# Low parts of all weights by a negated copy and a DMA that adds the weights from DRAM, low-part matmuls last, small first loads on other queues

## The chip, the cores and the metric

The kernel runs on one core of a Trainium2 chip. The metric is the device time of one execution in microseconds, the median of several runs. The profile is of one further execution.

## The reference

Two layers of a hybrid backbone are computed, for 128 context tokens and 512 latent tokens together (640 columns). Each layer modulates and normalises its input, projects it once to 11264 columns, and feeds four branches: a depthwise convolution of width 31, a Hyena long convolution, a pooling mixer and grouped-query attention.

```python
mod = jax.nn.silu(cond) @ p['w_ada'] + p['b_ada']
shift, scale, gate = jnp.split(mod, 3, axis=-1)
h = rms_norm(x, p['norm_g']) * (1.0 + scale) + shift
u = h @ p['w_in']
...
ya = (ya * jax.nn.silu(a_gate)) @ p['wo_conv']
yb = (yb * jax.nn.silu(b_gate)) @ p['wo_hyena']
yc = (yc * jax.nn.silu(c_gate)) @ p['wo_pool']
yd = (att * jax.nn.silu(d_gate)) @ p['wo_attn']
gm = jax.nn.sigmoid(g_merge).reshape(B, L, N_BRANCH, D_MODEL)
merged = gm[:, :, 0] * ya + gm[:, :, 1] * yb + gm[:, :, 2] * yc + gm[:, :, 3] * yd
return x + gate * (merged @ p['w_out'])
```

All inputs and outputs are float32.

## The kernel before

**Precision.** Every float32 operand of a large matmul is kept as two float32r parts, a high part (a rounded copy) and a low part (the operand minus its high part). A product takes three matmuls for each block of 128 rows: high weight with high activation, high weight with low activation, low weight with high activation. `proj` (L383) does that for a column weight: its output has the weight's 128 columns on the partitions and 320 of the 640 tokens, so `both` calls it twice for each weight. `token_proj` (L412) does it the other way round, with tokens on the partitions, for keys, values, queries and the output projection.

**Weights.** `weights` (L331) brings one weight: SyncE's queue loads it into a raw tile (`raw`, two buffers of 512 KB), ScalarE copies it rounded into `whi`, and the low part goes to `wlo` (three buffers each of `whi` and `wlo`). A flag, `pooled[0]`, chooses how. When it is false, VectorE subtracts (`raw` minus `whi`). When it is true, ScalarE writes minus `whi` into `wlo`, and a DMA issued by GpSimd adds `raw` to it. The flag is false for the first three weights of layer 0 (L1811, then true from L1825), true through the Hyena, attention and convolution inputs, and false from the end of the convolution's LayerNorm (`norm`, L1646) to the end of the layer (L1882, L1889). In one execution there are 272 such weights: 168 of eight 128x128 blocks, 56 of four, 40 of four blocks by 256 columns for `token_proj`, and 8 single blocks of the pooling branch. A weight of eight blocks takes 48 matmuls of 320 columns, one of four blocks 24.

**Order of work.** TensorE's order is written out by a small planner, `Loom` (L76): the branches are generators, each `yield` lets another one place its matmuls, and a model of the engines' times decides which goes next. The model only sets the order; it waits for nothing. The other engines' instructions are ordered by the framework's scheduler by priority, those of `weights` 120 instructions ahead (`WAHEAD`). Each engine's queue runs in order. The main line of a layer (`layers`, L1799) is: Hyena inputs and gates, values, keys, queries, the Hyena merge, convolution inputs, pooling inputs, the attention merge, the pooling branch's gates (an eight-block weight alternates with a single block), the pooling merge, the convolution's gates, the convolution's merge, and the output projection. In a merge a column weight of `w_in` (eight blocks) alternates with a column of the branch's own output weight (four blocks, eight for attention). Beside it run threads for the Hyena filters and convolutions, whose elementwise work is on VectorE, ScalarE and GpSimd.

**The start.** Before the planner runs, all first loads are issued on SyncE's queue in the order of the string `DORD`: digits are the eight chunks of `w_ada` (1 MB each, in two halves), `x` the tokens, `t` the Hyena tables, `f` to `i` filter parts. Nineteen small loads, the list `small` (seven of the filter network, the selector, ten parameter rows, one edge table), are dealt in between by `load_small` (L1929). `load` (L324) also gives the planner an estimate of each arrival.

Of the kernel before, what the change touches and what calls it, by code (L numbers as in the profile page):

```python
# [10 lines left out]
F32R = mybir.dt.float32r  # L11
I32 = mybir.dt.int32
AF = mybir.ActivationFunctionType
ALU = mybir.AluOpType
# [14 lines left out]
NSLOT = 13  # L29
NRAW = 2  # L30
NHI = 3
DORD = "0sf4xt15gh2637"
SMALL = 3
PT = 6.5
PN = 4.0
HW = 80
# [30 lines left out]
def r32(ap):  # L67
    return ap.bitcast(F32)
# [165 lines left out]
def hybrid_flow_backbone(ctx: ExitStack, tc: tile.TileContext, i, o):  # L234
    nc = tc.nc
# [85 lines left out]
            dve.scalar_tensor_tensor(out=lo, in0=src, scalar=scale, in1=r32(hi),  # L321
                                     op0=ALU.mult, op1=ALU.subtract)

    def load(dst, src):  # L324

        sp.dma_start(out=dst, in_=src)  # L326
        lm.issue = max(lm.issue, lm.pe - 2.0) + 0.48
        lm.dma = max(lm.dma, lm.issue + 1.2) + int(np.prod(dst.shape)) * 4 / 360e3
        return lm.dma + 1.9

    def weights(src, kk, n):  # L331
        yield from wr.get()
        lm.bg = True
        with tc.high_priority(offset=WAHEAD):
            raw = wp.tile([P, 1024], F32, tag="raw", name=nm("raw"), bufs=NRAW)
            hi = wp.tile([P, 1024], F32R, tag="whi", name=nm("whi"), bufs=NHI)
            lo = wp.tile([P, 1024], F32R, tag="wlo", name=nm("wlo"), bufs=NHI)
            w = kk * n
            rv = raw[:, 0:w]
            sp.dma_start(out=rv.rearrange("p (k c) -> p k c", k=kk), in_=src)  # L340
            act.copy(hi[:, 0:w], rv)
            if pooled[0]:

                act.activation(out=lo[:, 0:w], in_=r32(hi[:, 0:w]), func=AF.Copy, scale=-1.0)
                nc.gpsimd.dma_start(out=r32(lo[:, 0:w]), in_=rv, accum_op=ALU.add)  # L345
            else:
                dve.tensor_tensor(out=lo[:, 0:w], in0=rv, in1=r32(hi[:, 0:w]), op=ALU.subtract)
        lm.bg = False
        return (hi[:, 0:w].rearrange("p (k c) -> p k c", k=kk),
                lo[:, 0:w].rearrange("p (k c) -> p k c", k=kk))  # L350
# [32 lines left out]
    def proj(ps, w, c0, a, ks, j):  # L383

        whi, wlo = w
        n = len(ks)
        cols = slice(320 * j, 320 * j + 320)
        for m, (kw, ka) in enumerate(ks):
            wh, wl = whi[:, kw, c0:c0 + 128], wlo[:, kw, c0:c0 + 128]
            if a.ev:  # L390
                yield a.ev[ka]
            ah, al = a.h(ka)[:, cols], a.l(ka)[:, cols]
            pe.matmul(ps, wh, ah, start=(m == 0), stop=False)
            pe.matmul(ps, wh, al, start=False, stop=False)
            pe.matmul(ps, wl, ah, start=False, stop=(m == n - 1))
            if m % 2 == 1 and m < n - 1:
                yield

    def both(w, c0, a, nk, fn):

# [11 lines left out]
    def token_proj(src, a, fn):  # L412


        bank = {}
        for kh in range(2):
            whi, wlo = yield from weights(src[512 * kh:512 * kh + 512].rearrange("(k p) c -> p k c", p=P), 4, 256)
            for t in (1, 2, 3, 4, 0):
                b = (t + 1) // 2
                first = kh == 0 and t in (0, 1, 3)  # L420
                if first:
                    bank[b] = yield from mm.get()
                else:
                    yield
                out = bank[b][:, 0:256] if t in (0, 1, 3) else bank[b][:, 256:512]
                cols = slice(128 * t, 128 * t + 128)
                for k in range(4):
                    ah, al = a.h(4 * kh + k)[:, cols], a.l(4 * kh + k)[:, cols]
                    last = kh == 1 and k == 3
                    for n, (x, y) in enumerate(((ah, whi), (al, whi), (ah, wlo))):  # L430
                        pe.matmul(out, x, y[:, k, :], start=(first and k == 0 and n == 0),
                                  stop=(last and n == 2), skip_group_check=True)
                if t == 0:
                    wr.put(WD)
                if kh == 1 and t in (0, 2, 4):
                    if t:
                        yield from fn(t - 2, bank[b].rearrange("p (t c) -> p t c", t=2))
                    else:
                        yield from fn(-1, bank[b][:, 0:256].unsqueeze(1))
                    mm.put()  # L440
# [1087 lines left out]
    class Conv:  # L1528
# [58 lines left out]
        def norm(self):  # L1587

            l = self.l
            yield self.ev_tap  # L1590
            co = self.co
            pm = yield from sc.get()
            for j in range(2):
                pe.matmul(pm[:, j, 0:328], lnw.to_broadcast([P, P]), self.pad.v(328 * j, 328), start=True, stop=True)
            self.pad.free()
            for c in range(4):
                x = co.v(656 * c, 656)
                xh = x.rearrange("p (a b) -> p a b", a=2)
                yield turn
                dve.tensor_tensor(out=xh, in0=xh, in1=pm[:, :, 0:328], op=ALU.subtract)  # L1600
            sc.put()
            for c in range(4):
                sq = yield from ur.get(656)
                act.activation(out=sq, in_=co.v(656 * c, 656), func=AF.Square)
                if c == 0:
                    total = sq
                else:
                    dve.tensor_tensor(out=total, in0=total, in1=sq, op=ALU.add)
                    ur.put()
            yield lm.sync()  # L1610
            pvv = yield from ax.get()
            for t in range(5):
                t0 = 0 if t == 0 else 143 + 128 * (t - 1)
                pe.matmul(pvv[:, t:t + 1], total[:, t0:t0 + 128], lnw, start=True, stop=True)
            ur.put(0.0)
            v = sm.tile([P, 5], F32, tag="lnv", name=nm("lnv"))
            rs = sm.tile([P, 5], F32, tag="lnr", name=nm("lnr"))
            dve.tensor_scalar(out=v, in0=pvv[:, 0:5], scalar1=EPS, scalar2=None, op0=ALU.add)
            ax.put()
            rsqrt(rs, v, 5)  # L1620
            yield lm.sync()
            pr = yield from sc.get()
            for t in range(5):
                dst = pr[:, 1, 0:128] if t == 0 else pr[:, 0, 128 * (t - 1):128 * t]
                pe.transpose(dst, rs[:, t:t + 1].to_broadcast([P, P]), ident)
            self.sa = sa = yield from new_act(1)
            for c in range(4):
                x = co.v(656 * c, 656)
                xn = yield from ur.get(T)
                dve.tensor_tensor(out=xn[:, 0:128], in0=x[:, 0:128], in1=pr[:, 1, 0:128], op=ALU.mult)  # L1630
                yield turn
                dve.tensor_tensor(out=xn[:, 128:640], in0=x[:, 143:655], in1=pr[:, 0, :], op=ALU.mult)
                yield turn
                dve.tensor_scalar(out=xn, in0=xn, scalar1=par(l, c, R_LNG), scalar2=par(l, c, R_LNB),
                                  op0=ALU.mult, op1=ALU.add)
                th = yield from ur.get(T)
                act.activation(out=th, in_=xn, func=AF.Tanh, scale=0.5)
                yield turn
                dve.scalar_tensor_tensor(out=xn, in0=th, scalar=1.0, in1=xn, op0=ALU.add, op1=ALU.mult)
                ur.put()  # L1640
                split(sa.h(c), sa.l(c), xn, 0.5)
                ur.put()
            sc.put()
            co.free()
            self.ev_norm.set()
            pooled[0] = False  # L1646

        def gated(self):
            l = self.l
# [149 lines left out]
    def layers():  # L1799
# [4 lines left out]
        for l in range(DEPTH):  # L1804
# [74 lines left out]
            if l + 1 < DEPTH:  # L1879
                lm.spawn(late_filters(l + 1, ev_late[l]), 7)  # L1880
                lm.spawn(ada_later([(1, j) for j in range(8, 12)], 0.0, GS), 50, LATA)
            pooled[0] = False  # L1882
            if l + 1 < DEPTH:
                xT = yield from slots(2)
                evs = [Event(lm) for _ in range(4)]
            yield from out_proj(l, ma, xs, ssq, rows, xT, evs)
            for _ in range(2):
                ur.put()
            pooled[0] = False  # L1889
            ma.free()  # L1890
            if l + 1 < DEPTH:
                yield evs[3]
# [33 lines left out]
    h0 = hys[0]  # L1926
    xs0 = [Slot(), Slot()]

    def load_small(n):  # L1929

        for dst, src, t in small[:n]:
            t[0] = load(dst, src)
        del small[:n]

    def load_chunk(j):

# [9 lines left out]
            halves = [v[:, 0:4], v[:, 4:8]]  # L1946
        for kh in range(2):
            t = load(halves[kh], w_ada(0, j)[:, 4 * kh:4 * kh + 4])
            load_small(SMALL)
        chunks.append((j, s, halves, t))  # L1950

    for x in DORD:
        if x == "x":
            x_first = (xs0, sm.tile([P, 5, 2], F32, tag="ssq0", name=nm("ssq")),
                       load_x(xs0, i["x_prompt"][0], i["x_sample"][0]))
            load_small(2 * SMALL)
        elif x in "fghi":
            c, q = divmod("fghi".index(x), 2)
            if c not in h0.flt:
# [1 line left out]
            h0.fetch(c, q)  # L1961
        elif x == "t":
            h0.tables(Slot())
            load_small(2 * SMALL)
        elif x == "s":
            load_small(7)
        else:
            load_chunk(int(x))
    load_small(len(small))
    t_hid, t_prm = t_hid[0], t_prm[0]  # L1970
    lm.spawn(cond(s_cond, t_cond), 0)
    lm.spawn(hidden(s_hid, t_hid), 1)
# [102 lines left out]
```

## Time and profile before

| | |
|---|---|
| median of 3 runs | 2303.33 us (2302.43 to 2305.74) |
| the profiled execution | 2302.68 us |
| its span, first to last instruction | 2300.9 us |
| mean granted TensorE clock | 0.98 |
| TensorE, VectorE, ScalarE, GpSimd busy | 96%, 62%, 48%, 15% |
| bytes read from HBM, written | 174.34 MB, 12.22 MB |

The profile names an instruction by engine (PE is TensorE's matmuls, PEld its weight loads, DVE VectorE, ACT ScalarE, POOL GpSimd, SPq the queue of SyncE), by line and by its tiles as out<-in. Most operations go through helpers, so that their line is the helper's (L179 for elementwise work, L194 for matmuls, L203 for transposes, L326 for loads, L340 for the raw weights, L345 for the accumulating DMA), and the tile's name tells what they are. A busy TensorE isn't TensorE at its peak, as matmuls overlap. Idle time of an engine that others don't wait for costs nothing.

### The profile page before, as it was taken

The numbers are of one execution on the slowest core, as the hardware profiler recorded it, in microseconds if no ns is written. First come the engines' busy times: TensorE is split into PE (matmuls) and PEld (weight loads), VectorE is DVE, ScalarE is ACT, GpSimd is POOL, SyncE is SP. The second block draws the span as 40 slices with busy tenths as digits, with TensorE's granted clock in tenths as the row PEclk, the third lists the DMA queues.
The fourth block names the chain that finished last, engine by engine and source line by source line (L and its number), as shares of the span: only waits on it lengthen the run. The fifth ranks groups of instructions, "written<-read, shape, count | busy, mean of one in ns | idle before, by whom it ended". The sixth has DMA issues, their size and how long they took to land.

```text
span 2300.9 us, 39784 instructions
## 1 busy us (share of the span) xinstructions
PE 2201.6 (96%) x15951; PEld 2154.2 (94%) x15951; DVE 1416.2 (62%) x2853; ACT 1104.7 (48%) x2078; POOL 348.8 (15%) x348
## 2 busy tenths in 40 slices
PE   5998999999999999999989999999999999999999
PEld 3998999999999998999979999999999999899999
DVE  5785786556669854334466668756656897533433
ACT  4644456666664334223355453667667433422321
POOL 1633211000001111000045242000000111100000
PEclk8999999999999999999999999999999999999999
DMA  8465564444446655233545434444344576432332
GB/s 273 117 153 135 132 167 105 104 101 99 116 115 150 150 123 120 76 95 87 168 129 120 115 87 118 105 109 102 81 102 100 141 151 153 105 100 78 97 105 79
DMA packets 310440, 274.08 MB, mean 119 GB/s; under 512 B 11293, under 2 KB 279773, under 8 KB 309998
## 3 DMA queue, kind: packets, MB, share of 16 engines
q1 hardware_dynamic: 284622, 186.59, 26.9%
q0 software_dynamic: 25632, 84.95, 20.2%
q8 instruction: 125, 2.05, 0.4%
q14 instruction: 61, 0.50, 0.1%
HBM read 174.34 MB, written 12.22 MB: 81 GB/s over the span
## 4 chain that ended last, share of the span: by engine, by line
PE 75%; DVE 12%; DMA 5%; ACT 3%; issue 3%; POOL 1%; SPq 1%; POOLq 0%; ACTq 0%; DVEq 0%
PE mm L194 60%; DVE sl L179 6%; PE ax L194 6%; PE sc L194 5%; PE ax L203 4%; DVE wx L179 2%; DMA wlo<-raw 2%; DMA raw<-in_w_in_dram 1%; DVE k L179 1%; ACT u L179 1%; POOL sl L179 1%; SPq L326 1%; DVE u L179 1%; ACT wlo L179 1%; DMA sl<-in_hy_w_dram 1%
## 5 line engine op out<-in xcount | busy, mean ns | idle before, releaser
L194 PE MATMUL mm<-sl,whi 128*128 128x320 f32 x6304 | 1427.2, 314 | 7.7 <-DVE t L179 5.5
L194 PEld LDWEIGHTS mm<-sl,whi 128*128 128x128 f32 x6304 | 1058.1, 190 | 15.1 <-DVE t L179 4.8
L194 PE MATMUL mm<-sl,wlo 128*128 128x320 f32 x3152 | 982.8, 312 | 6.8 <-DMA wlo<-raw 5.9
L194 PEld LDWEIGHTS mm<-sl,wlo 128*128 128x128 f32 x3152 | 597.5, 190 | 7.6 <-DMA wlo<-raw 6.4
L179 ACT CAST whi<-raw 128x1024 fp32r<-128x1024 f32 (+2 forms) x272 | 255.4, 939 | 581.8 <-PE mm L194 419.8
L345 POOL DMA_DIRECT2D wlo<-raw x178 | 154.6, 868 | 1140.9 <-ACT wlo L179 844.3
L194 PE MATMUL mm<-whi,sl 128*128 128x256 f32 x1600 | 289.8, 283 | 0.0
L194 PEld LDWEIGHTS mm<-whi,sl 128*128 128x128 f32 x1600 | 244.9, 188 | 1.6 <-issue 0.8
L179 DVE TENSOR_TENSOR wlo<-raw,whi 128x1024 fp32r<-128x1024 f32 x94 | 95.6, 1017 | 225.1 <-ACT whi L179 224.8
L194 PE MATMUL mm<-wlo,sl 128*128 128x256 f32 x800 | 224.1, 280 | 0.8 <-DMA wlo<-raw 0.8
L194 PE MATMUL sc<-sl,sl 128*128 128x128 f32 (+1 forms) x1344 | 208.4, 298 | 10.2 <-DVE sl L179 3.9
L179 DVE SCALAR_TENSOR_TENSOR sc<-sl,prm,sc 128x640 f32<-128x640 f32 (+14 forms) x232 | 207.2, 893 | 11.2 <-ACT sc L179 6.7
L179 DVE TENSOR_TENSOR h<-ax,h 128x512 fp32r<-128x512 f32 (+1 forms) x200 | 120.6, 604 | 131.3 <-ACT h L179 130.2
L194 PEld LDWEIGHTS sc<-sl,sl 128*128 128x128 f32 x1344 | 182.4, 197 | 13.6 <-DVE u L179 5.2
L179 ACT ACTIVATE wlo<-whi 128x1024 fp32r<-128x1024 f32 (+2 forms) x178 | 174.6, 981 | 1.6
L179 DVE SCALAR_TENSOR_TENSOR t<-t,mm 128x320 f32<-128x320 f32 x192 | 93.1, 485 | 133.2 <-PE mm L194 101.5
L179 ACT ACTIVATE t<-mm 128x320 f32<-128x320 f32 x208 | 89.9, 432 | 130.8 <-PE mm L194 130.5
L194 PEld LDWEIGHTS mm<-wlo,sl 128*128 128x128 f32 x800 | 150.8, 189 | 1.0 <-DMA wlo<-raw 1.0
L179 ACT CAST h<-ax 128x512 fp32r<-128x512 f32 (+1 forms) x200 | 102.5, 514 | 70.4 <-PE ax L203 68.3
L179 DVE TENSOR_SCALAR_CACHE_REDUCE u<-sc,rq 128x640 f32<-128x640 f32 x128 | 112.7, 880 | 38.0 <-PE sc L194 36.7
L194 PE MATMUL ax<-h,sl 128*128 128x256 f32 (+1 forms) x656 | 121.8, 298 | 4.8 <-DVE h L179 4.5
L179 ACT ACTIVATE u<-u,nb 128x640 f32<-128x640 f32 x128 | 106.2, 829 | 37.8 <-DVE u L179 37.0
(194 smaller groups left out, 2208.8 us busy)
## 6 DMA issues: line engine op xcount, KB each, us to landing
raw<-in_w_in_dram SPq DMA_DIRECT2D x176, 512.0 KB
wlo<-raw POOLq DMA_DIRECT2D x152, 512.0 KB, 4.7
wlo<-in_w_ada_dram SPq DMA_DIRECT2D x19, 512.0 KB
whi<-in_w_ada_dram SPq DMA_DIRECT2D x19, 512.0 KB
raw<-in_wo_attn_dram SPq DMA_DIRECT2D x16, 512.0 KB
raw<-in_w_out_dram SPq DMA_DIRECT2D x16, 512.0 KB
sl<-in_c_decay_dram SPq DMA_DIRECT2D x16, 320.0 KB
mscr<-t SPq DMA_DIRECT2D x16, 320.0 KB
```

What stands on the lines that cost most here:

```text
L179: r = f(*args, **kw)
L194: r = self.real.matmul(out, lhsT, rhs, **kw)
L203: r = self.real.transpose(out, in_, ident)
L326: sp.dma_start(out=dst, in_=src)
L345: nc.gpsimd.dma_start(out=r32(lo[:, 0:w]), in_=rv, accum_op=ALU.add)
```

## The change

Four things are changed.

- The accumulating DMA takes its addend from the weight in DRAM, in the same arrangement of blocks as the first load, and no longer from `raw`. Its destination is the same low part, now as float32r.
- The three places that set the flag to false at the end of `norm` and around the output projection are gone. The line that sets it at the beginning of a layer stays, so the first three weights of layer 0 are still subtracted on VectorE.
- `proj` and `token_proj` do all matmuls with the high part of the weight first, and those with its low part after them. The places at which other threads may cut in move: after every third block of the high part, and before every fourth block of the low part.
- The small loads at the start leave SyncE's queue: the first seven are issued by ScalarE's, the other twelve by GpSimd's, all ahead of the planner's run. `DORD` loses its `s`.

```diff
-DORD = "0sf4xt15gh2637"
-SMALL = 3
+DORD = "0f4xt15gh2637"
...
-    def load(dst, src):
-
-        sp.dma_start(out=dst, in_=src)
+    def load(dst, src, eng=None):
+
+        (eng or sp).dma_start(out=dst, in_=src)
+        if eng:
+            lm.dma = max(lm.dma, lm.pe + 1.2) + int(np.prod(dst.shape)) * 4 / 360e3
+            return max(lm.dma + 1.9, 12.0)
...
                 act.activation(out=lo[:, 0:w], in_=r32(hi[:, 0:w]), func=AF.Copy, scale=-1.0)
-                nc.gpsimd.dma_start(out=r32(lo[:, 0:w]), in_=rv, accum_op=ALU.add)
+                nc.gpsimd.dma_start(out=lo[:, 0:w].rearrange("p (k c) -> p k c", k=kk), in_=src.bitcast(F32R),
+                                    accum_op=ALU.add)
...
         for m, (kw, ka) in enumerate(ks):
-            wh, wl = whi[:, kw, c0:c0 + 128], wlo[:, kw, c0:c0 + 128]
             if a.ev:
                 yield a.ev[ka]
-            ah, al = a.h(ka)[:, cols], a.l(ka)[:, cols]
-            pe.matmul(ps, wh, ah, start=(m == 0), stop=False)
-            pe.matmul(ps, wh, al, start=False, stop=False)
-            pe.matmul(ps, wl, ah, start=False, stop=(m == n - 1))
-            if m % 2 == 1 and m < n - 1:
+            wh = whi[:, kw, c0:c0 + 128]
+            pe.matmul(ps, wh, a.h(ka)[:, cols], start=(m == 0), stop=False)
+            pe.matmul(ps, wh, a.l(ka)[:, cols], start=False, stop=False)
+            if m % 3 == 2 and m < n - 1:
                 yield
+
+        for m, (kw, ka) in enumerate(ks):
+            if m % 4 == 0:
+                yield
+            pe.matmul(ps, wlo[:, kw, c0:c0 + 128], a.h(ka)[:, cols], start=False, stop=(m == n - 1))
...
-                for k in range(4):
-                    ah, al = a.h(4 * kh + k)[:, cols], a.l(4 * kh + k)[:, cols]
-                    last = kh == 1 and k == 3
-                    for n, (x, y) in enumerate(((ah, whi), (al, whi), (ah, wlo))):
-                        pe.matmul(out, x, y[:, k, :], start=(first and k == 0 and n == 0),
-                                  stop=(last and n == 2), skip_group_check=True)
+                for n, (part, y) in enumerate(((a.h, whi), (a.l, whi), (a.h, wlo))):
+                    for k in range(4):
+                        pe.matmul(out, part(4 * kh + k)[:, cols], y[:, k, :], start=(first and k == 0 and n == 0),
+                                  stop=(kh == 1 and k == 3 and n == 2), skip_group_check=True)
...
             self.ev_norm.set()
-            pooled[0] = False
...
-            pooled[0] = False
             if l + 1 < DEPTH:
                 xT = yield from slots(2)
...
-            pooled[0] = False
             ma.free()
...
-    def load_small(n):
-
-        for dst, src, t in small[:n]:
-            t[0] = load(dst, src)
-        del small[:n]
+
+    for n, (dst, src, t) in enumerate(small):
+        t[0] = load(dst, src, nc.scalar if n < 7 else nc.gpsimd)
```

The calls of `load_small` between the large loads go with it.

## Rows read from the trace of the kernel before

**Rows 1.** The page's engine line: busy us, share of the span, instructions.

```profile
PE 2201.6 (96%) x15951; PEld 2154.2 (94%) x15951; DVE 1416.2 (62%) x2853; ACT 1104.7 (48%) x2078; POOL 348.8 (15%) x348
```

**Rows 2.** Busy time by stretch; columns as in the first line, GB/s last.

```profile
core 0: us, PE busy (x) PEld busy (x) DVE busy (x) ACT busy (x) POOL busy (x), PEclk, DMA share, GB/s
850.00:900.00 50.00, 42.39 (x257) 41.09 (x256) 30.73 (x65) 23.52 (x41) 6.96 (x8) 0.90 0.50 113
950.00:1000.00 50.00, 50.00 (x342) 50.00 (x341) 18.46 (x27) 11.91 (x19) 0.00 (x0) 1.00 0.28 80
1100.00:1150.00 50.00, 50.00 (x405) 49.69 (x404) 21.50 (x30) 21.43 (x47) 0.00 (x0) 1.00 0.55 176
```

**Rows 3.** TensorE's waits in the whole span: us in total, times, longest.

```profile
PE ax L203 <- DVE sl L179: 21.1, 7, 5.9
PE ax L194 <- DMA wlo<-in_w_ada_dram: 9.2, 1, 9.2
PE ax L203 <- DMA sl<-in_x_prompt_dram: 7.0, 1, 7.0
PE mm L194 <- DMA wlo<-raw: 6.7, 3, 3.3
...
PE ax L194 <- POOL sl L179: 5.5, 2, 3.5
```

**Rows 4.** Timelines of SyncE, ScalarE, GpSimd and TensorE, 883 to 897 us: start, duration.

```profile
883.65 0.37 SPq L340 DMA_DIRECT2D raw<-in_w_in_dram  x1
...
887.96 1.05 ACT L179 CAST whi<-raw 128x1024 fp32r<-128x1024 f32 x1 [2.34 <-DMA raw<-in_w_in_dram]
...
889.55 1.05 ACT L179 ACTIVATE wlo<-whi 128x1024 fp32r<-128x1024 f32 x1
...
890.89 0.87 POOL L345 DMA_DIRECT2D wlo<-raw  x1 [6.86 <-ACT wlo L179]
...
896.87 0.48 PE L194 MATMUL mm<-sl,wlo 128*128 128x320 f32 x1 [2.58 <-DMA wlo<-raw]
```

**Rows 5.** Busy time by stretch at the start.

```profile
7.50:10.00 2.50, 2.08 (x17) 0.50 (x10) 0.00 (x0) 0.16 (x1) 0.00 (x0) 1.00 0.23 42
10.00:12.50 2.50, 2.21 (x4) 0.87 (x3) 0.25 (x1) 1.50 (x2) 0.00 (x0) 1.00 0.67 181
12.50:15.00 2.50, 0.00 (x0) 0.00 (x0) 2.40 (x4) 0.00 (x0) 0.00 (x0) 1.00 0.40 96
...
42.50:45.00 2.50, 2.16 (x17) 0.47 (x13) 0.46 (x5) 1.18 (x3) 1.08 (x1) 0.50 1.07 357
```

**Rows 6.** Timeline of SyncE's queue at the start: start, duration of the issue.

```profile
2.31 0.45 SPq L326 DMA_DIRECT2D sl<-in_c_zfeat_dram  x1
...
5.16 1.45 SPq L326 DMA_DIRECT2D sl<-in_hy_w_dram  x2
...
16.14 0.39 SPq L326 DMA_DIRECT2D edge<-in_c_edge_dram  x1
...
19.39 2.23 SPq L326 DMA_DIRECT2D wlo<-in_w_ada_dram  x1
```

**Rows 7.** Instructions on the low parts: ns least/median/most, first and last start.

```profile
L345 POOL DMA_DIRECT2D wlo<-raw x178: 850/869/1024, 93.0 to 2019.6; - x178
...
L179 DVE TENSOR_TENSOR wlo<-raw,whi x94: 691/1217/1927, 58.8 to 2275.2; 128x1024 fp32r<-128x1024 f32 x56, 128x512 fp32r<-128x512 f32 x38
```

**Rows 8.** Stretches with one 64 KB accumulation, and with one raw load, alone.

```profile
862.30:863.00 0.70, 0.70 (x7) 0.70 (x6) 0.48 (x2) 0.00 (x0) 0.00 (x0) 0.96 0.85 94
955.00:959.00 4.00, 4.00 (x29) 4.00 (x28) 0.02 (x1) 1.05 (x3) 0.00 (x0) 1.00 0.44 131
```

**Rows 9.** The page's DMA issues: count, size, median us from issue to landing.

```profile
wlo<-raw POOLq DMA_DIRECT2D x152, 512.0 KB, 4.7
...
wlo<-raw POOLq DMA_DIRECT2D x8, 64.0 KB, 2.8
```

**Rows 10.** The page's DMA queues: packets, MB, share of 16 engines.

```profile
q0 software_dynamic: 25632, 84.95, 20.2%
```

**Rows 11.** GpSimd's instructions by shape: busy us, mean ns, idle before.

```profile
L179 POOL TENSOR_TENSOR sl<-sl 128x640 f32<-128x640 f32 x32 | 56.2, 1756 | 9.7 <-DVE sl L179 9.7
```

More of the change, by code (lines that the diff above doesn't have):

```diff
@@ L1948, in load_chunk @@
             t = load(halves[kh], w_ada(0, j)[:, 4 * kh:4 * kh + 4])
-            load_small(SMALL)
         chunks.append((j, s, halves, t))
@@ L1955, in hybrid_flow_backbone @@
                        load_x(xs0, i["x_prompt"][0], i["x_sample"][0]))
-            load_small(2 * SMALL)
         elif x in "fghi":
@@ L1963, in hybrid_flow_backbone @@
             h0.tables(Slot())
-            load_small(2 * SMALL)
-        elif x == "s":
-            load_small(7)
         else:
             load_chunk(int(x))
-    load_small(len(small))
     t_hid, t_prm = t_hid[0], t_prm[0]
```

## The prediction, made before the change was run

> **What bounds the kernel now.** I read the engine table first: TensorE is busy for 2201.6 of 2300.9 us, 96%, VectorE for 62%, ScalarE for 48%, GpSimd for 15% [rows 1]. So only the idle 99 us, and what the clock loses after idle stretches, can be won; work taken off another engine wins nothing where TensorE doesn't wait for it. The table by stretches then says where the idle time is [rows 2]. From 950 to 1000 us, and likewise in the other ends of the layers, TensorE is busy for all 50 us with 342 matmuls, 0.146 us each, at full clock. Those stages can only lose. From 850 to 900 us it is busy for 42.4 us at a granted clock of 0.90.
>
> Third, TensorE's waits [rows 3]: 9.2 and 7.0 us at the start, for the first big loads; 21.1 us for VectorE in the Hyena part; 5.5 us for GpSimd; and 6.7 us for the low parts that the accumulating DMA makes. The events around one of the last kind say why [rows 4]: the raw load starts only at 883.65, though its target had been copied long before, because the accumulation of the weight two places earlier still reads that buffer. The raw weights reach ScalarE at 887.96, the negation runs at 889.55, GpSimd issues at 890.89, and the low part is there at 896.87, after TensorE has waited 2.58 us. So in this stage two raw buffers held until the accumulation lands are the limit, not any engine.
>
> The start is another story [rows 5, 6]. Of the 19 small loads SyncE's queue issues the first at 2.31 and the last at 16.14 us; most issues take 0.25 to 0.58 us, one pair 1.45. In 7.5 to 15 us the DMA engines are busy for 0.23, 0.67 and 0.40. At 19.39 an issue first takes 2.23 us, and from then on the DMA is full (1.07 at 42.5 us). Before 19 us issuing is the limit, after it the bytes.
>
> **Part 1, small loads elsewhere.** 19 issues leave SyncE: seven go to ScalarE's queue, twelve to GpSimd's. The big loads move up. Worth: the idle DMA share of 7.5 to 15 us, (0.77 + 0.33 + 0.60) x 2.5 = 4.3 us; at most the 19 issues' own time, about 8 us. What they are moved past: on ScalarE the first tanh for the conditioning waits behind seven issues, some 3 us by the same 0.25 to 0.58 each, and with it the first modulation matmuls, which have time, as later chunks of the same sum arrive until 50 us; on GpSimd twelve issues at 0.87 [rows 7] are 10 us, and its first other work is at 44 us. I take -4.3, with -8 and +3 as ends. The Trainium skill (DMA: Bandwidth & Descriptors, Issuing engines are not separate DMA queues) says that spreading issues over engines saves only the sequencer's time and is usually small. The trace agrees from 19 us on and not before it. By the rule alone this term would be about 0 and the sum 2298.
>
> **Part 2, raw buffer free earlier.** The accumulation reads DRAM, so raw is free after ScalarE's copy. The three waits of 6.7 us [rows 3] lose their cause. A stall also costs clock: 0.90 over 50 us is 10 us at the lower level, 1.2 of 2.4 GHz, around three stalls, 3.3 us each, in which half the work is lost, 1.7 us. Two of the waits are long enough (2.6 and 3.3 us). Together 6.7 + 3.4 = 10.1 us, if nothing else is late next.
>
> **Part 3, is the low part late?** 91 more of the 272 low parts come by this way: 94 are subtracted on VectorE now [rows 7], and only the first three stay there, since the flag is still false when layer 0 begins. VectorE loses some 90 us, ScalarE gets about 76 (53 of 1.05 us [rows 4] and 38 of half the size), mostly in stages where it is busy for 12 to 15 of 50 us: hidden, as TensorE waits for neither there. Cover gone, a full ScalarE would delay evictions; it stays under 60%.
>
> What is new is the shape: 1024 pieces of 512 B where there were 128 of 4 KB. Transfer: a 64 KB accumulation in 512 B pieces keeps the 16 engines busy for 0.85 x 0.70 = 0.60 us, its queue's closing packets and a few others included [rows 8]; eight of them less closings are 4.5 us. Large pieces land after 4.7 us and 64 KB after 2.8 [rows 9], so 512 KB moves in 0.6 + 1.9 = 2.5 us now. The new landing is 4.7 - 2.5 + 4.5 = 6.7 us, plus what more pieces cost GpSimd in writing. That cost no row shows: an issue takes 0.85 to 1.02 us for every size, but always with 128 pieces [rows 7]. Bounds: 0.87 us if all of it is fixed, 8 x 0.87 = 6.95 if all of it goes by pieces. Half and half gives 3.9; I take 2.4, halfway from there to the fixed end, the only one a row stands at. So landing after 8.2 us. The Trainium skill (DMA: Bandwidth & Descriptors, Anatomy of one DMA) calls descriptor generation small and says that many can be emitted before it shows. No run here tests that. With its price nothing is added, and the sum would be about 2 us lower.
>
> From the release of a weight's slot to its low part: 1.05 + 1.05 (copy, negation) + 0.3 hand-over + 8.2 = 10.6 us. Time there is: in a merge (8-block weight of 48 matmuls, then 4-block of 24) the slot was left one pair earlier, 72 x 0.146 = 10.5 us; low parts last adds 16 matmuls, 2.35 us: 12.9. It holds with 2.3 us to spare; the break-even is 4.7 us of writing. Where 8-block weights alternate with the pooling branch's 64 KB ones, there are 54 x 0.146 + 2.35 = 10.3 us: 0.3 late at 8 places, +2 us. With only 8-block weights it is 16.4 us. Matmuls and weight loads are as many as before and each matmul has its own load in both orders, so I give the order itself no cost. It adds places where other threads may cut in (four instead of three a half weight), which moves stalls both ways; I take 0, between -4 and +4.
>
> DMA room: q0 goes from 25632 packets to some 220,000 [rows 10]. A raw 512 KB load takes 0.44 x 4.0 = 1.76 us of all engines [rows 8]. A merge pair needs 1.5 x (1.76 + 4.5) = 9.4 of 10.5 us, 90%. At the layer boundary (share 0.55 now without any accumulation, [rows 2]), eight w_out weights in 1 KB pieces, by the two piece sizes some 3.3 us each, add about 27 us in 50, a share of 1.09 in all: just over full. I give +2 us there, between 0 and +8.
>
> GpSimd's queue is in order: a negation that is late, or 1.5 us more writing, now stands before its sums for the filters (1.76 us each, [rows 11]), for which TensorE already waits 5.5 us. With a weight per 10 us there, a collision in one of six and half of it hidden: +2 us, bounds 0 and +20.
>
> **Sum.** The profiled execution took 2302.68 us, its span 2300.9; the median is 2303.33, so 0.65 is added. -4.3 - 10.1 + 2 + 2 + 2 = -8.4: 2294.3, +0.65, about 2295.
>
> **Rivals.** (1) The forecast, 2284 to 2298.7, chance 0.49: waits for low parts vanish, the start moves up. (2) No change, 2302, 0.17: the earlier loads only make VectorE the limit at 60 to 75 us, and the low-part gain is eaten by new waits of the same size; for it speaks that the Hyena waits (21.1 + 5.5 us, a quarter of the idle time) aren't touched. (3) Slower by GpSimd, 0.20: writing goes by pieces. From 4.7 us on, each merge pair (48 in the merges, 8 before the conv's gate) is late by the excess. Halfway, at 5.8 us: 56 x 1.1 + 8 x 3.7 = 91, with the start's gain 2390; at 6.95 about 2460. Against it: pieces of 512 B to 4 KB cost the same. (4) Slower by the DMA engines, 0.14: pieces from DRAM cost more than from SBUF. Break-even in a pair is 10.5/1.5 - 1.76 = 5.2 us, 82 ns a piece against 70; the end is 70 plus 27, a plain read's piece (1.76 x 16 / 1024). There a pair takes 11.9 us, 56 x 1.4 = 78, and 32 weights of the attention merge 0.9 more each: about 2400; halfway 2350.
>
> **Numbers.** 2295. The range takes in the forecast, no change and the nearer half of the slower cases: 2284 to 2375; outside it lie 0.05 below and about 0.14 above. A measurement of this kernel tells 0.2% (4.6 us) from no change. Faster 0.49, same 0.17, slower 0.34, from the four cases in order.
>
> **What would show it.** Right: no waits of TensorE for low parts, big loads issued before 10 us, first projection some 4 us earlier, GpSimd's issues of 1024 pieces under 4.7 us, landings of 8 us or less, full TensorE from 950 to 1100 and 2050 to 2250 us. Wrong: issues over 4.7 us, a DMA share near 1 in the ends of the layers with low-part waits there, or longer waits for VectorE and GpSimd in the Hyena part.

## The result, and the profile of the changed kernel

The changed kernel takes 2285.47 us (median, 2283.87 to 2286.45), the kernel before 2303.64 us on the same chip: a ratio of 0.9919, 95% interval 0.9902 to 0.9937, some 18 us less. 2295 was predicted, a gain of 8.4; the time lies 1.5 us above the lower end of the range. The profiled execution took 2285.64 us, its span is 2283.8.

First the engine line and the line of the accumulating DMA's queue of the changed kernel's page. They answer to [rows 1, 10].

```profile
PE 2192.5 (96%) x15951; PEld 2145.5 (94%) x15951; DVE 1333.8 (58%) x2762; ACT 1190.4 (52%) x2169; POOL 590.2 (26%) x451
...
q0 software_dynamic: 223856, 122.96, 42.4%
```

VectorE lost 82 us and ScalarE got 86. GpSimd has 103 instructions more and 241 us more. TensorE's idle time went from 99.3 to 91.3 us.

The same stretches as in [rows 2, 5] (us, busy times of TensorE, its weight loads, VectorE, ScalarE and GpSimd, granted clock, DMA share, GB/s):

```profile
7.50:10.00 2.50, 1.01 (x8) 0.92 (x8) 1.21 (x1) 0.91 (x2) 0.24 (x1) 1.00 1.14 302
10.00:12.50 2.50, 2.44 (x17) 1.09 (x18) 0.00 (x0) 0.38 (x2) 0.00 (x0) 1.00 1.14 272
12.50:15.00 2.50, 2.50 (x8) 1.31 (x7) 0.54 (x1) 0.00 (x0) 0.00 (x0) 1.00 1.08 355
...
850.00:900.00 50.00, 46.60 (x312) 45.41 (x313) 29.52 (x64) 26.77 (x43) 13.16 (x10) 1.00 0.84 149
950.00:1000.00 50.00, 50.00 (x342) 50.00 (x341) 11.32 (x20) 20.52 (x30) 13.54 (x10) 1.00 0.86 147
1100.00:1150.00 50.00, 47.52 (x390) 46.75 (x389) 14.20 (x24) 24.55 (x49) 7.72 (x6) 1.00 0.97 228
```

From 850 to 900 us TensorE does 312 matmuls instead of 257, at full clock instead of 0.90. From 950 to 1000 us nothing is lost, with a DMA share of 0.86 instead of 0.28. At the layer's end, 1100 to 1150, the DMA is full and 2.5 us go idle that were not before. At the start the DMA engines are full in all three stretches.

GpSimd's issues of the accumulation answer to [rows 7] (ns least/median/most, first and last start):

```profile
L347 POOL DMA_DIRECT2D wlo<-in_w_in_dram x173: 1273/1559/2866, 98.8 to 2199.9; - x173
L347 POOL DMA_DIRECT2D wlo<-in_wo_hyena_dram x16: 1282/1294/1304, 333.3 to 1680.7; - x16
L347 POOL DMA_DIRECT2D wlo<-in_pool_w_dram x8: 890/896/906, 844.4 to 1997.5; - x8
```

The page's DMA issues answer to [rows 9] (count, size, median us from issue to landing):

```profile
wlo<-in_w_in_dram POOLq DMA_DIRECT2D x173, 512.0 KB, 6.5
...
wlo<-in_w_out_dram POOLq DMA_DIRECT2D x16, 512.0 KB, 7.2
```

And TensorE's waits, the largest, beside [rows 3]:

```profile
PE ax L193 <- ACT k L178: 12.6, 2, 11.5
PE ax L202 <- DVE sl L178: 10.1, 4, 8.8
PE mm L193 <- DMA wlo<-in_w_in_dram: 4.9, 3, 3.0
```

The two waits for low parts at the pooling gates, 2.58 and 3.31 of the 6.7 us, are gone. Waits for low parts are not: 1.04 us at 305 us stands where 0.77 was, 3.00 at 1551 us in layer 1's Hyena merge is new, 0.85 at 2147 us is new, and the output projection's weights add one of 1.50 at 1110 us. At the start the 9.2 us for a first chunk have become 3.2 and the 7.0 us for the tokens are gone, but the first wait, for VectorE, is 8.8 instead of 5.9 us. There is one wait of 11.5 us that the kernel before did not have.

The kernel before had two more gaps at the pooling gates, put down to VectorE: 2.58 us at 883.98 and 1.74 at 2010.65, within the first line. The lines below it, of ScalarE, VectorE and TensorE, lead up to the longer one:

```profile
PE mm L194 <- DVE t L179: 5.5, 6, 2.6
...
876.13 1.05 ACT L179 CAST whi<-raw 128x1024 fp32r<-128x1024 f32 x1 [3.36 <-DMA raw<-in_w_in_dram]
...
877.85 0.83 DVE L179 SCALAR_TENSOR_TENSOR sl<-u,sl 128x640 fp32r<-128x640 f32 x1 [2.76 <-ACT sl L179]
...
883.98 0.90 PE L194 MATMUL mm<-sl,whi 128*128 128x320 f32 x2 [2.58 <-DVE t L179]
```

ScalarE stands for 3.36 us at the copy of a raw weight that is loaded late, VectorE then waits 2.76 us for ScalarE, and TensorE for VectorE.

To see where the time went I cut both traces at the same marks (the first projection, first and last store of the Hyena merge, the LayerNorm's transposes, first and last store of the output). What lies between a layer's first projection and the first store of its Hyena merge is called its Hyena part. For each piece I added TensorE's idle time and half of the time at the lower clock level, 1.2 of 2.4 GHz. The sums differ by 17.1 us, which is the difference of the spans. That works because both kernels spend about as long at the lower level before the first projection, 20.5 and 21.5 us. There it costs little that shows: in the run with the flag as before it doesn't occur before the first projection at all, which yet starts only 0.7 us earlier. The piece from the LayerNorm to the first output store (pooling gates, merges, conv gates) goes from 10.9 to 3.4 us in layer 0 and from 9.0 to 2.2 in layer 1: 14.3 us of the 17.1. Up to the first projection it is 36.3 to 34.3. The largest other changes are in layer 1: 3.1 us more lost in its Hyena part and 5.0 less in the Hyena merge; no other piece changes by over 2.

### The profile page after: what moved, and what is told of

Same layout as the page of the kernel before. It is cut to its first block, busy times and chain, and to the rows that moved or that the text cites. A ratio compares the mean times of both kernels' runs of the same rounds, so it can differ in the third digit from the quotient of the medians.

```text
span 2283.8 us, 39935 instructions
## 1 busy us (share of the span) xinstructions
PE 2192.5 (96%) x15951; PEld 2145.5 (94%) x15951; DVE 1333.8 (58%) x2762; ACT 1190.4 (52%) x2169; POOL 590.2 (26%) x451
## 4 chain that ended last, share of the span: by engine, by line
PE 74%; issue 9%; DVE 8%; POOL 4%; ACT 3%; DMA 2%; ACTq 0%; SPq 0%; POOLq 0%; DVEq 0%
PE mm L193 58%; PE sc L193 6%; PE ax L193 6%; DVE sl L178 4%; PE ax L202 4%; POOL wlo L347 2%; POOL sl L178 1%; DMA sl<-in_hy_w_dram 1%; DMA wlo<-in_w_in_dram 1%; DVE wx L178 1%; DVE k L178 1%; ACT sl L178 0%; DVE t L178 0%; ACT u L178 0%; DVE u L178 0%
## 5 line engine op out<-in xcount | busy, mean ns | idle before, releaser
L193 PE MATMUL mm<-sl,whi 128*128 128x320 f32 x6304 | 1053.9, 312 | 9.6 <-DVE sl L178 3.9
L193 PEld LDWEIGHTS mm<-sl,whi 128*128 128x128 f32 x6304 | 948.1, 188 | 14.8 <-DVE sl L178 4.5
L193 PE MATMUL mm<-sl,wlo 128*128 128x320 f32 x3152 | 553.7, 311 | 0.9 <-DMA wlo<-in_w_in_dram 0.9
L347 POOL DMA_DIRECT2D wlo<-in_w_in_dram x173 | 264.9, 1531 | 860.2 <-ACT wlo L178 599.5
L193 PEld LDWEIGHTS mm<-sl,wlo 128*128 128x128 f32 x3152 | 483.3, 188 | 1.9 <-DMA wlo<-in_w_in_dram 1.1
L178 ACT ACTIVATE wlo<-whi 128x1024 fp32r<-128x1024 f32 (+2 forms) x269 | 254.9, 948 | 35.6 <-PE mm L193 32.7
L193 PE MATMUL mm<-whi,sl 128*128 128x256 f32 x1600 | 228.8, 286 | 4.2 <-ACT u L178 2.1
L193 PE MATMUL mm<-wlo,sl 128*128 128x256 f32 x800 | 128.3, 283 | 5.5 <-DMA wlo<-in_w_in_dram 4.0
L202 PE MATMUL ax<-ident,u 128*128 128x128 f32 x752 | 118.6, 273 | 3.6 <-DVE h L178 2.0
L193 PEld LDWEIGHTS mm<-wlo,sl 128*128 128x128 f32 x800 | 109.3, 190 | 6.3 <-DMA wlo<-in_w_in_dram 4.5
```

The lines of the kernel that those rows point to most:

```text
L178: r = f(*args, **kw)
L193: r = self.real.matmul(out, lhsT, rhs, **kw)
L202: r = self.real.transpose(out, in_, ident)
L347: nc.gpsimd.dma_start(out=lo[:, 0:w].rearrange("p (k c) -> p k c", k=kk), in_=src.bitcast(F32R), accum_op=ALU.add)
```

## Experiments

Each kernel is one of the two, with one edit. The parts of the change are called **start** (small loads on other queues), **DRAM** (the addend), **order** (low parts last) and **flag** (no more subtraction on VectorE in the layers' ends). Ratios are to the kernel before on the same chip, with 95% intervals. TensorE's matmuls come in the same order in the kernel before and in DRAM alone; in order alone and in DRAM with order; and in the changed kernel, the one with the addend from the raw buffer and the two with more issues. Between kernels of one such group the planner's order is no cause of a difference.

**The start alone** in the kernel before.

```diff
-DORD = "0sf4xt15gh2637"
+DORD = "0f4xt15gh2637"
...
+    for n, (dst, src, t) in enumerate(small):
+        t[0] = load(dst, src, nc.scalar if n < 7 else nc.gpsimd)
```

> The kernel before with only the start changed (19 small loads on ScalarE's and GpSimd's queues). Theory: the big loads move up, the first projection starts some 5.5 us earlier as in the changed kernel (53.1 against 58.8 us), but part of that is filter work done later, so the time falls by 2 to 6 us: 2298 to 2302. Rival (the start gains nothing, VectorE is the limit at 60 to 75 us): within 2 us of 2303.6.

Measured: 2307.35 us, 1.0014 [1.0005, 1.0023]. The first projection matmul starts at 52.90 us instead of 58.78, as meant, but the first store of the Hyena merge comes at 361.0 instead of 357.9, and the span ends 5.8 us later. What is won at the start is lost again up to the Hyena merge, and the stalls at the pooling gates stay. The filters' work and the planner's order are likely causes of the loss; the run doesn't tell them apart.

**The DRAM addend alone** in the kernel before.

```diff
-                nc.gpsimd.dma_start(out=r32(lo[:, 0:w]), in_=rv, accum_op=ALU.add)
+                nc.gpsimd.dma_start(out=lo[:, 0:w].rearrange("p (k c) -> p k c", k=kk), in_=src.bitcast(F32R),
+                                    accum_op=ALU.add)
```

> The kernel before with only the addend of the accumulating DMA taken from DRAM; the flag, the order of matmuls and the start as before. Theory: the raw buffer was the limit, so the TensorE gaps at 881 to 897 us and 2008 to 2023 us (2.6 + 2.6 and 1.7 + 3.3 us, with the clock behind them) go, 10 to 14 us: 2290 to 2294. Rival (low parts last or the flag took them away): the gaps stay or grow by the longer landing (6.5 against 4.7 us), 2303 or more.

Measured: 2304.81 us, 1.0002 [0.9991, 1.0014]: nothing. The timelines of SyncE, ScalarE, GpSimd and TensorE at the pooling gates say why:

```profile
893.41 1.04 ACT L179 CAST whi<-raw 128x1024 fp32r<-128x1024 f32 x1
...
894.47 0.39 SPq L340 DMA_DIRECT2D raw<-in_w_in_dram  x1
...
895.04 1.04 ACT L179 ACTIVATE wlo<-whi 128x1024 fp32r<-128x1024 f32 x1
...
896.48 1.57 POOL L345 DMA_DIRECT2D wlo<-in_w_in_dram  x1 [2.40 <-ACT wlo L179]
...
905.52 0.61 PE L194 MATMUL mm<-sl,wlo 128*128 128x320 f32 x1 [3.16 <-DMA wlo<-in_w_in_dram]
```

The raw buffer is reloaded right behind its copy, at 894.47, and the gaps in which TensorE had waited for VectorE have shrunk to 0.30 us, with TensorE's order unchanged. So the held raw buffer was the cause of those as well. But the low part now needs 12.1 us from the copy to its matmul, as this accumulation lands 8.9 us after its issue (the median is 6.4), and it is late by 3.16 us here and 3.52 at the same place of layer 1. The first limit is removed and the next stands right behind it.

**The order alone** in the kernel before.

```diff
+            pe.matmul(ps, wh, a.h(ka)[:, cols], start=(m == 0), stop=False)
+            pe.matmul(ps, wh, a.l(ka)[:, cols], start=False, stop=False)
...
+            pe.matmul(ps, wlo[:, kw, c0:c0 + 128], a.h(ka)[:, cols], start=False, stop=(m == n - 1))
```

> The kernel before with only the order of matmuls changed (low parts last). Theory: the low part is needed 2.35 us later, so waits of 2.6 and 3.3 us for it shrink to under 1 us and lose their clock, but the raw buffer still turns around too slowly and the waits beside them stay: 4 to 9 us, 2295 to 2300; the planner's other order in the Hyena part may add 5 us either way. Rival (the order alone is the cure): 12 us or more, 2291 or less.

Measured: 2307.1 us, 1.0021 [1.0008, 1.0034]. The waits for low parts at the gates shrink to 1.03 and 0.58 us in layer 0 and 0.20 in layer 1, those for VectorE stay (1.80 and 1.94), and layer 0's Hyena part is 20 us later at its merge's first store (378.3 against 357.9), most of which is won back by the end. The order of the filters' matmuls is another one there, since the places to cut in have moved.

**DRAM and order together** in the kernel before (both edits above).

> The kernel before with two parts together: the accumulating DMA reads DRAM, and low-part matmuls come last; the start and the three places of the flag as before. Theory (the two parts need each other): alone the DRAM source came to 2304.8 because the low part then landed late by 3.2 and 3.5 us, and alone the new order came to 2307.1 with VectorE's gaps of 1.8 and 1.9 us left. Together the four gaps in the pooling gates (before: 10.2 us idle and some 4 us of clock) vanish, and the Hyena part stays where it was: 2288 to 2295, with no TensorE wait over 1 us from the Hyena merge to the first store of the output in either layer. Rival A (the flag carries it: VectorE's relief in the tails): 2302 to 2308, gaps on VectorE stay. Rival B (the planner's order decides): the pooling gates gain their 14 us, and the Hyena part loses 5 to 15 as it did in the run of the new order alone: 2295 to 2305.

Measured: 2290.02 us, 0.9945 [0.9933, 0.9958]. By the ratios the two came alone to +0.5 and +4.8 us, together to -12.7. Against order alone that is 17.5 us less with the same order of matmuls, so they are the addend's and not the planner's. Of the 14.1 us between the two profiled spans, 10.1 lie in layer 0's Hyena part, and 2.0 and 4.9 between the LayerNorm and the first output store; the other pieces give 2.9 back. At the gates TensorE no longer stands:

```profile
886.52 2.59 PE L194 MATMUL mm<-sl,whi 128*128 128x320 f32 x16 [0.29 <-DVE t L179]
...
889.61 1.42 PE L194 MATMUL mm<-sl,wlo 128*128 128x320 f32 x8 [0.49 <-DMA wlo<-in_w_in_dram]
```

Sixteen matmuls with the high part run before the first with the low part, and the wait left is 0.49 us. Idle time and half of the lower-clock time from the LayerNorm to the first output store are 3.6 and 1.4 us: all of the 14.3 us that the changed kernel wins there, and it is won without flag and start. Two things were not as expected: the first store of layer 0's Hyena merge comes 11 us later than in the kernel before (368.8 against 357.9), and one wait of 3.01 us for a low part stands in layer 1's Hyena merge.

**The changed kernel with the flag as before.**

```diff
             self.ev_norm.set()
+            pooled[0] = False
```

(and the same at the two other places).

> The changed kernel with the three places of the flag restored, so that the low parts of the layers' ends are subtracted on VectorE again (94 of them); everything else as changed. Theory: from the pooling gates on TensorE waits for nothing in either way, because the new order and the earlier raw buffers cover VectorE's subtraction too; within 4 us of the changed kernel: 2282 to 2292. Rival A (the flag carries the gain): the gaps on VectorE at the pooling gates (2.6 and 1.7 us before) come back and the time goes to 2292 to 2300.

Measured: 2283.26 us, 0.9911 [0.9896, 0.9927], no worse than the changed kernel. VectorE is busy for 1429.4 us again and TensorE doesn't mind. The 91 low parts taken off VectorE are worth nothing.

**The changed kernel with the old order** (three matmuls of a block side by side).

```diff
+            pe.matmul(ps, wh, ah, start=(m == 0), stop=False)
+            pe.matmul(ps, wh, al, start=False, stop=False)
+            pe.matmul(ps, wl, ah, start=False, stop=(m == n - 1))
```

> The changed kernel with the three matmuls of a block side by side again, as before the change. Theory: the landing from DRAM takes 6.3 to 6.5 us after an issue of 1.55 us, and without the 2.35 us that the order gives it comes late where 8-block weights alternate with single blocks and at each merge pair by up to 1 us: TensorE waits for low parts in the merges, the pooling gates and the conv's gates; 2295 to 2320. Rival (the order is worth nothing beside the DRAM source): 2283 to 2290. Rival B (the planner's order of the Hyena part moves the time by 5 to 10 us either way) shows as a difference before the Hyena merge's first store in both layers, and is read from the stages.

Measured: 2330.49 us, 1.0121 [1.0107, 1.0136]. TensorE's waits for low parts:

```profile
PE mm L193 <- DMA wlo<-in_w_in_dram: 31.8, 15, 7.1
```

More than expected, and at another place. A wait at each merge pair doesn't come: the slot's cycle is 2.4 + 6.5 = 8.9 us against 10.5 us of a pair, so most pairs hold without the order. Of the 15 waits, ten are in the Hyena parts and the Hyena merges. The Hyena parts are also planned in another order there, so the 45 us are not the price of the waits alone; the two were not separated.

**The changed kernel with the old start.**

```diff
-DORD = "0f4xt15gh2637"
+DORD = "0sf4xt15gh2637"
...
+    load_small(len(small))
```

> The changed kernel with the start of before: small loads on SyncE's queue. Theory: the first projection matmul falls back by 5.7 us to about 58.8, and some of that is lost again in the Hyena part, where VectorE and the filters set the end: 2287 to 2292. The prediction's own term (4.3 us on the path): 2289 to 2290. Rival (the start is worth nothing or costs, as in the run of the new start alone, 2307.4 against 2303.9): 2280 to 2285.

Measured: 2292.87 us, 0.9960 [0.9948, 0.9973]: the start is worth 0.41% or some 9 us by the ratios, 7.4 by the medians. From DRAM with order (0.9945) to the same with the start (0.9911) it is 0.34%. In all three pairs the first projection moves by 5.9 to 7.1 us; what the end sees of it is -9, -8 or, in the kernel before, +3 us. How the Hyena part takes it differs, and the planned order differs in each of the three pairs.

**The changed kernel with the addend from the raw buffer.**

```diff
+                nc.gpsimd.dma_start(out=r32(lo[:, 0:w]), in_=rv, accum_op=ALU.add)
```

> The changed kernel with the addend taken from the raw buffer in SBUF again; all low parts by the DMA, low parts last, start as changed. Theory: a raw buffer turns around in some 13 us for an eight-block and 8 us for a four-block weight, so two buffers just carry a merge pair of 10.5 us; waits come back in the pooling branch's gates and some in the ends of the layers: 2295 to 2312. Rival (the flag and the order are the gain): 2285 to 2289.

Measured: 2343.75 us, 1.0175 [1.0161, 1.019], far more than expected. The waits are mostly in the layers' ends and short, but for one of 6.5 us at the output projection:

```profile
PE mm L193 <- DVE t L178: 16.9, 17, 6.5
PE mm L193 <- DMA wlo<-raw: 12.4, 18, 1.7
```

The stretch from 950 to 1000 us of the same kernel:

```profile
950.00:1000.00 50.00, 47.80 (x313) 45.70 (x313) 8.57 (x15) 18.57 (x30) 8.60 (x10) 1.00 0.60 132
```

Where the changed kernel does 342 matmuls in 50 us, this one does 313. With all low parts by the accumulation, two raw buffers held until it lands don't suffice in a merge. TensorE's order is the changed kernel's, so all of the 59 us between the two (by the ratios) are the addend's place. So the flag is not a gain by itself, but it is only affordable with the DRAM addend.

**More writing on GpSimd**: each accumulation of the changed kernel issued as four, then as eight DMAs, same bytes, same pieces. The diff is the eight's; the four have `kk // 4`.

```diff
+                lv = lo[:, 0:w].rearrange("p (k c) -> p k c", k=kk)
+                st = max(1, kk // 8)
+                for k0 in range(0, kk, st):
+                    nc.gpsimd.dma_start(out=lv[:, k0:k0 + st], in_=src[:, k0:k0 + st].bitcast(F32R),
+                                        accum_op=ALU.add)
```

> The changed kernel with each accumulation issued as four DMAs of a quarter of the blocks each, same bytes and same pieces: GpSimd's writing for an eight-block weight goes from 1.56 us to about 4 x 1.05 = 4.2 us by its issues of 128 and 512 pieces (0.90 and 1.29 us). The prediction's break-even was 4.7 us of writing in a merge pair. Theory (the break-even holds, at the landing as measured it is rather 5.5): no new waits for low parts in the merges; GpSimd's sums for the filters are late at some places: 2285 to 2300. Rival (there is no slack left after the change, each us of writing is paid at the 56 merge pairs): 2.6 x 56 = 146 us, about 2430.

> The changed kernel with each accumulation issued as eight DMAs of one block of 128 rows each (128 pieces, 0.90 us each by the issues for single blocks): writing takes 7.2 us for an eight-block weight, close to the far end 6.95 us of the prediction's slower rival, which gave 2460 there. Theory (the prediction's pair rule): the slot's cycle is 2.4 (copy, negation, hand-over) + 7.2 + 4.9 (landing of the last) = 14.5 us against 12.9 of a merge pair, and GpSimd is busy for 1.5 x 7.2 = 10.8 of 10.5 us a pair; late by 0.3 to 1.6 us at each of 56 pairs and by more at the pooling gates, plus the filters' sums behind a full queue: 2320 to 2460. Rival (pieces of one block land one by one and matmuls of block k wait for block k alone, so that it is hidden): 2285 to 2300.

Measured: four 2302.46 us, 0.9988 [0.9975, 1.0002]; eight 2347.1 us, 1.0186 [1.0171, 1.0201]. The page's groups of the issues for `w_in` (count, busy us, mean ns of one, idle before), of the four:

```profile
L350 POOL DMA_DIRECT2D wlo<-in_w_in_dram x692 | 825.1, 1941 | 486.7 <-ACT wlo L178 383.7
```

of the eight:

```profile
L350 POOL DMA_DIRECT2D wlo<-in_w_in_dram x1288 | 1259.4, 2543 | 315.1 <-ACT wlo L178 232.1
```

and the stretch from 950 to 1000 us, in the merges, of the eight:

```profile
950.00:1000.00 50.00, 50.00 (x342) 50.00 (x341) 9.50 (x16) 19.09 (x27) 50.00 (x60) 1.00 0.90 151
```

825.1 / 173 weights is 4.8 us of writing a weight, at the predicted break-even of 4.7; 1259.4 / 173 is 7.3 (7.8 for a weight of eight issues, as some have four), beyond the predicted rival's far end. From the LayerNorm to the first output store the four cost 3.1 us in layer 0 and 1.0 in layer 1, the eight 11.2 and 9.3. A break-even of a merge pair shows at neither: in the last row GpSimd is busy for 50 of 50 us and TensorE still does its 342 matmuls, and in these pieces the eight cost 20 us and not 2.6 x 56 = 146. Their waits for low parts there add up to 12.4 us, but none lies between 905 and 1041 us, where layer 0's pooling merge runs. Neither run is the prediction's case of one long issue, though: here the first blocks land while the later ones are still being written. Of the rest of the loss, 16.2 and 11.6 us for the eight and 6.0 and 2.0 for the four come up to the Hyena merge of layer 0 and in the Hyena part of layer 1, where GpSimd's sums for the filters stand in the same queue: VectorE's waits for them total 14.5 us in the changed kernel, 17.3 in the four and 36.0 in the eight. TensorE's order is the same in all three kernels.

**The new wait of 11.5 us.** In the changed kernel TensorE stands at a filter matmul; its table is issued late (timelines of SyncE and TensorE):

```profile
1205.42 0.57 SPq L325 DMA_DIRECT2D sl<-in_c_decay_dram  x1
1206.04 0.63 SPq L325 DMA_DIRECT2D sl<-in_hy_w_dram  x1
...
1209.97 0.58 PE L193 MATMUL ax<-k,hd 128*128 128x256 f32 x1 [11.50 <-ACT k L178]
```

The stretch ahead of it:

```profile
1190.00:1205.00 15.00, 8.47 (x48) 8.21 (x47) 14.48 (x28) 9.01 (x18) 5.76 (x5) 0.73 0.72 117
```

VectorE is busy for 14.48 of 15 us ahead of it, and the table's slot comes free behind that work: SyncE's queue waits 8.0 us for VectorE before the issue at 1205.42. If the planner only placed the matmul too early, a later estimate should help. The edit:

```diff
-                self.ld[c, q] = t
+                self.ld[c, q] = t + (8.0 if l else 0.0)
```

> The changed kernel with one edit of the planner: in layer 1 the arrival of the filter's first tables is estimated 8 us later, so that the planner places the filter's matmuls later and projection matmuls before them. Theory: the stall of 11.5 us at 1198 us, where TensorE stands at filter matmuls whose table SyncE could load only at 1206, shrinks to under 4 us, at most 11.5 + some clock: 2272 to 2281. Rival (the layer's beginning is bound by VectorE, which is busy for all of 1184 to 1208 us, and the wait only moves to another instruction): 2283 to 2290.

Measured: 2291.73 us, 0.9943 [0.9931, 0.9956], 6 us more than the changed kernel. The wait is gone, and in its place stand

```profile
1194.20 0.79 PE L193 MATMUL ax<-k,hd 128*128 128x256 f32 x2 [5.28 <-DVE sl L178]
...
1204.49 0.58 PE L193 MATMUL ax<-ones,k 128*128 128x1 f32 x2 [5.78 <-POOL k L178]
```

11.06 us in two pieces, on VectorE and on GpSimd. The rival's mechanism fits, though the time is 1.7 us above its range too: VectorE is busy for 19.31 of the 21 us from 1185 to 1206 us, and where the wait shows is the planner's choice. That an edit of one estimate moves the time by 6 us also says how far a run with another planned order can be off for no other reason.

## Why the prediction was right, point by point

The forecast's mechanism and sign were right: raw buffers free earlier, with the low parts last to cover the longer way. Its size, 8.4 of 18 us, was less than half, and a gain 1.5 us larger would have left the range. The terms:

- **Start, -4.3 (-8 to +3).** The DMA share of 7.5 to 15 us went from 0.23, 0.67, 0.40 to 1.14, 1.14, 1.08, and the first projection moved by 5.7 us, so the mechanism is as told. In the end times the kernels with it are 7 to 9 us faster with DRAM and order and 3 slower without. As the planned order differs in each pair, and another order alone moved the time by 6 us, how much of that is the earlier loads is not shown. The term was treated as independent of the rest, which it is not.
- **Raw buffer, -10.1.** Mis-sized in two ways. The two gaps on VectorE at the gates (2.58 and 1.74 us) had the same cause, as the DRAM addend alone shows, and were not counted: four gaps of 10.2 us at the gates, where the sum has 6.7, of which 0.77 lay in the Hyena part and stayed. And the lower clock before was 10.2 and 6.8 us in the two pieces, worth 8.5 us, against 3.4 in the sum; after, there is none. Not all of it was the raw buffer's: it came in five stretches of 3.4 us, at 862.9, 883.4, 897.1, 1989.3 and 2023.5 us, and the first of each layer follows TensorE's wait of 1.87 or 2.98 us for the LayerNorm. Those waits are still there, 2.1 us each, and why the clock no longer falls behind them is open. The small new waits at the layer's end take some of it back: 14.3 us net.
- **Writing, 2.4 us taken (0.87 to 6.95).** Measured 1.56 us for 1024 pieces, 1.29 for 512, 0.90 for 128. The median landing is 6.5 us, not 8.2, but at the pooling gates, where the estimate was needed, eight-block weights land after 7.0 to 8.0 us, and 21 of 269 landings take over the 8 us that were named as a sign. The +2 us there didn't come all the same: the largest wait is 0.42 us, on VectorE. The Trainium skill (DMA: Bandwidth & Descriptors, Anatomy of one DMA) calls the generation of descriptors small; the trace agrees in kind, with 0.66 us for 896 more pieces.
- **The order itself, 0 (-4 to +4).** Alone it costs 4.8 us (1.8 to 7.8 by its interval), at or beyond that end. That DRAM needs it was in the sum as the 2.35 us of cover. The addend alone, 2304.8 us, shows that without this cover the whole of part 2 would have been lost.
- **DMA room.** 90% of a merge pair was predicted; measured 0.86 of 50 us, in which 342 matmuls are 4.75 pairs, or 9.05 us a pair against 9.4. At the layer's end 1.09 was predicted, +2 us; measured 0.97, with 1.5 us of waiting for the low parts of `w_out`. Between the first output store and the next layer's first projection 1.1 us more are lost.
- **GpSimd's queue, +2 (0 to +20).** The waits for GpSimd of 5.5 us before are not among the changed kernel's largest any more, the longest is 0.5 us. The mechanism exists, as VectorE's waits for GpSimd in the eight issues show (36.0 against 14.5 us), but TensorE doesn't feel it at 1.56 us of writing.
- **VectorE relieved: hidden.** Right, the flag is worth nothing (2283.3 against 2285.5 us).
- **Rivals.** Slower by GpSimd asked for over 4.7 us of writing; it was 1.56. The pair rule charged all that was over to each of 56 pairs; issued in eight, at 7.3 us, the merges absorb a GpSimd that is busy all the time. For one issue of that length the rule is not tested. Slower by the DMA engines is ruled out by the pair's 9.05 us, less than by SBUF's price. No change by the start eaten in the Hyena part is what the start alone does, and it turned only in combination.

The sum came out lower than the gain because of the raw buffer's term and two charges of +2 us, at the gates and for GpSimd's queue, that didn't come; the start's share of the changed kernel's gain can't be read from stages, since the Hyena parts are planned anew with most edits.

What stays open: why the Hyena part gives the start's 6 us on in one planned order and not in another. The runs show that the end times differ so, and that an estimate 8 us later moves the time by 6.

## What to carry to other kernels

A buffer that is held for a slow step can be freed by letting that step read the original again; then look at once at the step that is next late, since here the addend from DRAM alone was worth nothing, the later use of its result alone cost 5 us, and both together gave 13. When stalls are counted, count all that have the same buffer behind them, whatever engine they are put down to, and the lower clock after each by its own rows. In a kernel whose order is planned by a model, a change of under 10 us needs the parts in combination, as the same edit gave +3 or -9 us.

## What the runs showed of the hardware that I had not expected

- An accumulating DMA in 1024 pieces of 512 B costs GpSimd 1.56 us to issue against 0.87 in 128 pieces of 4 KB [rows 7]: pieces cost, but far less than in proportion.
- Reading the addend from DRAM instead of SBUF made the queue no slower: a merge pair with it fits in 9.05 us of all DMA engines, under the estimate from the SBUF row [rows 8]. A 512 B piece of an accumulation takes a median of 65 ns of one DMA engine with the addend in SBUF (the kernel before) and in DRAM (the changed kernel); a plain one takes 27.
- Issues that follow each other on GpSimd overlap in the trace: with four a weight, 692 of a mean 1.94 us are 825 us of busy time, and a median of 1.74 us stands against a least of 0.85. With eight a weight, a 64 KB accumulation lands after a median of 5.0 us, against 2.8 alone [rows 9].
